# Spilled output products without the residual, and returning outputs on SyncE's queue, in a sparse-attention layer with its FFN

## The chip, the cores and the metric

The kernel runs on one core of a Trainium2 chip. Its time is the device time of one execution in microseconds (us). The time before is the median of 3 runs; a separate execution was taken by the hardware profiler, and its trace gives the rows that are quoted below. Lower is better.

## The reference

For 512 tokens of width 2048 in float32, one layer of a decoder trunk:

```
h = x + nsa_mixer(rmsnorm(x) * mix_g)            # 16 heads of 128, 4 key/value groups
h = h + swiglu(rmsnorm(h) * ffn_g)               # 2048 -> 2 x 5632 -> 2048
out = rmsnorm(h) * final_g
```

The mixer projects the normed tokens, computes for every head a compressed, a selected and a windowed attention with a position bias, adds the three with gates, and multiplies the joined heads by `nsa_w_out` (2048 x 2048). What matters here is the last step: `h = x + o @ nsa_w_out`, with `o` the 16 heads' outputs.

## The kernel before

**Number form.** Every product of two matrices is made from values split into a high part (written by ScalarE in the type that the rows call fp32r) and a low part (the rest, by VectorE): three matmuls for each product (`three`, L267 to L269). So weights arrive as `raw`, ScalarE writes `whi` (L97), VectorE `wlo` (L98). The class `Weights` does this in one fixed order of blocks (512 KB each) with 3 raw buffers: a new raw load may only be issued when VectorE has split an earlier block. During the attention these loads go through the queue of GpSimd (`W.queue = pool`), before and after it through SyncE's.

**The attention.** The loop over heads `h` has 12 steps each. A head's softmax rows (`P`) are scaled and transposed by VectorE in `finish` (L809 to L817), stored to DRAM in four pieces per token block by SyncE (`d_p`, L819), and fetched back turned (`ptr`, L823, SyncE); ScalarE and VectorE split them into `pth` and `ptl` (`turn`, L840 to L844), and TensorE multiplies them with the values (`values`, PSUM tile `o`). While one head is turned and multiplied, the next one's scores are made (`scores`, L802, L804). SyncE's queue also loads the bias rows (`tb`, L773) and stores the outputs of heads 0 to 11 (`d_o`, L865, from the one buffer `stage`).

**The dense stream.** Between the attention's matmuls, `pump` puts matmuls of a generator that runs through the projections of the later heads and then through `partial(0)` to `partial(3)`; the order of every engine's instructions is written by this program. The tiles `hn_h`, `hn_l` first hold the normed input, and, as soon as the last projection `qpair(14)` no longer reads a slice, the outputs of the heads: `reload_o(i)` (L698) loads output `i` from `d_o` into slice `i` of `hn_l`, and `split_o(k)` (L702, L703) splits the slices `2k`, `2k+1`. Reloads 0 to 8 are issued within the last projection, 9 to 11 in the first block of `partial(0)`; splits 0 and 1 come at the end of the projection, 2 to 5 within `partial(0)`.

**The spilled products.** The output projection has 2048 columns. For the first 1024 (`N_SPILL` = 4 chunks of 256), `partial(cb)` multiplies heads 0 to 11 while the last heads' attention still runs. It loads the residual `x` of these columns into `stage` (L712, GpSimd's queue), adds the finished PSUM halves to it (L728, VectorE, eight times in all), and stores the result in DRAM (`d_h`, L729, GpSimd).

**After the attention.** `acc` (512 x 2048) takes `x` for the last 1024 columns (L923) and `d_h` for the first 1024 (L924), both by SyncE. Then heads 0 to 11 are multiplied for the last 1024 columns (two blocks of 512, `cb` 2 and 3, six weight blocks each), added to `acc` (L928), then heads 12 to 15 for all columns, token block by token block, with the second norm (L977) behind each. The feed-forward part follows and takes the rest of the time.

The order around the change is that of the four queues: SyncE issues its transfers in program order and stops at each until what it waits for is there; GpSimd does the same for its own; ScalarE and VectorE work in order.

Of the kernel before, what the change touches and what calls it, by code (L numbers as in the profile page):

```python
# [10 lines left out]
F32 = mybir.dt.float32  # L11
F32R = mybir.dt.float32r
I32 = mybir.dt.int32
AF = mybir.ActivationFunctionType
OP = mybir.AluOpType
# [5 lines left out]
NT, KC = S // 128, D // 128  # L21
# [152 lines left out]
def nsa_block(ctx: ExitStack, tc: tile.TileContext, x, rel_bias, mix_g, ffn_g, fin_g, w_in, w_out,  # L174
              pos_k, w1k, w2k, pos_v, w1v, w2v, f_in, f_out, onehot, out):
    nc = tc.nc
    mm, act, dve, pool = nc.tensor.matmul, nc.scalar.activation, nc.vector, nc.gpsimd
# [17 lines left out]
    hn_h, hn_l = hn_t = [hnp.tile([128, KC, S], F32R, name=f"hn_{x}") for x in "hl"]  # L195
# [3 lines left out]
    d_o = [dram.tile([4, 128, S], F32, name=f"d_o{i}") for i in range(3)]  # L199
    d_h = dram.tile([S, 256 * N_SPILL], F32, name="d_h")  # L200
# [4 lines left out]
    def tok(t):  # L205
        return slice(128 * t, 128 * (t + 1))
# [22 lines left out]
    def rstd(ss):  # L229
        y = smallp.tile([128, 1], F32, name="rs")  # L230
        run(rstd_steps(ss, y))
        return y

    def scaled(src, y, gb, dst):
        for j in range(4):
            c = slice(512 * j, 512 * (j + 1))
            dve.scalar_tensor_tensor(dst[:, c], src[:, c], y, gb[:, c], op0=OP.mult, op1=OP.mult)
# [22 lines left out]
    def turned(xn, js, t):  # L260

        ps = transposed(xn, js, [ps3.tile([128, 512], F32, name="pp") for _ in js])
        his(ps, t, n2_hl)
        los(ps, t, to=n2_hl)

    def three(o, ah, al, bh, bl, start, stop):
        mm(o, ah, bh, start=start, stop=False, skip_group_check=True)  # L267
        mm(o, ah, bl, start=False, stop=False, skip_group_check=True)  # L268
        mm(o, al, bh, start=False, stop=stop, skip_group_check=True)  # L269
# [16 lines left out]
    def run(gen):  # L286
        for _ in gen:
            pass
# [61 lines left out]
    with ExitStack() as st1:  # L350
# [4 lines left out]
        def proj_tiles(n=2):  # L355
            return [(ps1 if next(turns) % 4 > 1 else psx).tile([128, 512], F32, name="proj") for _ in range(n)]
# [5 lines left out]
        with ExitStack() as st0:  # L362
# [28 lines left out]
            def bank(shape):  # L391
                return ps1.tile(shape, F32, name=next(names))
# [49 lines left out]
            p = bank([128, 512])  # L442
            for i in range(N_WARM):
                nc.tensor.transpose(p[:, 128 * (i % 4):128 * (i % 4 + 1)], ident, ident)
            p = bank([128, KC])
# [3 lines left out]
            ps = [bank([128, S]) for _ in range(4)]  # L449
# [5 lines left out]
            ps = proj_tiles()  # L455
            for q in range(4):
# [22 lines left out]
                if q == 3:  # L479
                    p = bank([128, S])  # L480
# [71 lines left out]
        ps = proj_tiles()  # L552
# [3 lines left out]
        ps = proj_tiles()  # L556
# [7 lines left out]
        ps, hk = proj_tiles(), ps1.tile([128, 256], F32, name="mlp")  # L564
# [8 lines left out]
        ps = proj_tiles()  # L573
# [5 lines left out]
        ps, hv = proj_tiles(4), ps1.tile([128, 256], F32, name="mlp")  # L579
        ge = cp.tile([128, NT, 3, H], F32, name="ge")  # L580
        for i in range(8):
# [10 lines left out]
            if i == 1:  # L592
                p = ps1.tile([128, 128], F32, name="tr")
# [16 lines left out]
        ps = proj_tiles()  # L610
# [10 lines left out]
        p = ps1.tile([96, G, 128], F32, name="tr")  # L621
# [8 lines left out]
    with ExitStack() as st2:  # L630
# [13 lines left out]
        def stage_tile():  # L644
            return ap_.tile([128, 1024], F32, name="stage", bufs=1)
# [3 lines left out]
        def proj2():  # L649
            pool_ = (psx, ps2)[next(units) % 2]  # L650
            return [pool_.tile([128, 512], F32, name="proj") for _ in range(2)]
# [43 lines left out]

        def reload_o(i):

            pool.dma_start(hn_l[:, i].bitcast(F32), d_o[i // 4][i % 4])  # L698

        def split_o(k):  # L700
            h, l = (x[:, 2 * k:2 * k + 2] for x in (hn_h, hn_l))
            act(h, l.bitcast(F32), AF.Copy)  # L702
            dve.tensor_tensor(l, l.bitcast(F32), h.bitcast(F32), op=OP.subtract)  # L703

        def partial(cb):
            st = stage_tile().rearrange("p (t c) -> p t c", t=NT)
            c = slice(256 * cb, 256 * (cb + 1))
            ps = [p.rearrange("p (t c) -> p t c", t=2) for p in proj2()]
            for i in range(3):
                w = W.take()  # L710
                if i == 1:
                    pool.dma_start(st, x[:, c].rearrange("(t p) c -> p t c", p=128))  # L712
                for t in range(NT):
                    if not cb and i == 0 and t < 3:
                        reload_o(9 + t)
                    if not cb and i < 2 and t % 2 == 0:
                        split_o(2 + 2 * i + t // 2)
                    if i == 2 and t == 2:
                        W.ahead(3)
                    for k in range(4):  # L720
                        h = 4 * i + k
                        three(ps[t // 2][:, t % 2], hn_h[:, h, tok(t)], hn_l[:, h, tok(t)], w[0][:, k], w[1][:, k],
                              h == 0 and t % 2 == 0, h == 11)
                        if k % 2:
                            yield 650
                    if i == 2 and t % 2:
                        b = t // 2
                        dve.tensor_tensor(st[:, 2 * b:2 * b + 2], st[:, 2 * b:2 * b + 2], ps[b], op=OP.add)  # L728
            pool.dma_start(d_h[:, c].rearrange("(t p) c -> p t c", p=128), st)  # L729
            done["n"] += 1  # L730
            yield None
# [189 lines left out]
    acc = accp.tile([128, NT, D], F32, name="acc")  # L921
    spill = 256 * N_SPILL
    nc.sync.dma_start(acc[:, :, spill:], x[:, spill:].rearrange("(t p) c -> p t c", p=128))  # L923
    nc.sync.dma_start(acc[:, :, :spill], d_h.rearrange("(t p) c -> p t c", p=128))  # L924

    def add(t, cb, p):
        a = acc[:, t, 512 * cb:512 * (cb + 1)]
        dve.tensor_tensor(a, a, p, op=OP.add)  # L928

    def tokmajor(po, w, lhs, first, last, t):  # L930
        for k in range(2):
            lh, ll = lhs(k)
            three(po, lh[:, tok(t)], ll[:, tok(t)], w[0][:, k], w[1][:, k], first and k == 0, last and k == 1)

    def out_tiles():
        return [psx.tile([128, 512], F32, name="proj") for _ in range(2)] + [
            ps3.tile([128, 512], F32, name="po", bufs=2) for _ in range(2)]

    def heads(i):
        return lambda k: (hn_h[:, 2 * i + k], hn_l[:, 2 * i + k])  # L940

    with tc.tile_pool(name="n2", bufs=1) as n2:
        act(warm, epsc, AF.Sqrt)
        gb2 = n2.tile([128, D], F32, name="gb2")
        nc.scalar.dma_start(gb2, ffn_g[0:1, :].to_broadcast([128, D]))
        xn = n2.tile([128, D + 64], F32, name="xn")
        wr_h = n2.tile([128, 6, 1024], F32R, name="wr_h")
        wr_l = n2.tile([128, 6, 1024], F32R, name="wr_l")
        for i in range(6):
            W.place[marks[0] + i] = wr_h[:, i], wr_l[:, i]  # L950
        for cb in (2, 3):
            po = out_tiles()
            for i in range(6):
                w = W.take(2 if cb == 2 else min(2 + i, 6))
                for t in range(NT):
                    tokmajor(po[t], w, heads(i), i == 0, i == 5, t)
            W.ahead(3)
            for t in range(NT):
                add(t, cb, po[t])
        w8 = []  # L960
        for t in range(NT):
            ss = smallp.tile([128, 4], F32, name="ss4")
            po = out_tiles()
            for cb in range(4):
                for i in range(2):
                    if t == 0:
                        w8.append(W.take(7 - len(w8)))
                    tokmajor(po[cb], w8[2 * cb + i], heads(6 + i), i == 0, i == 1, t)
                add(t, cb, po[cb])
                if t == NT - 1 and cb == 3:  # L970
                    W.ahead(3)
                if cb == 3:
                    pool.dma_start(d_r[t], acc[:, t])
                if t and cb in (1, 2):
                    turned(xn, (2 * cb - 2, 2 * cb - 1), t - 1)
                junk = ps3.tile([128, 512], F32, name="pp")
                act(junk, acc[:, t, 512 * cb:512 * (cb + 1)], AF.Square, accum_out=ss[:, cb:cb + 1])  # L977
            scaled(acc[:, t], rstd(ss), gb2, xn)
            W.ahead(min(t, 2))
        pa = [ps3.tile([128, 512], F32, name="pp") for _ in range(2)]  # L980
        gs = []
        for i in range(4):
            gs.append(W.take(min(2, 3 - i)))
            run(ws(pa, i, gs[i], 0, 256, of=n2_hl))
            if i in (1, 2):
                turned(xn, (2 * i - 2, 2 * i - 1), 3)
        act(warm, epsc, AF.Silu)
# [3 lines left out]
    hn_h, hn_l = n2_hl  # L991
# [293 lines left out]
    acc = late.tile([128, NT, D], F32, name="acc")  # L1285
# [171 lines left out]
    c = slice(1536, 2048)  # L1457
# [46 lines left out]
```

## Time and profile before

| | |
|---|---|
| median of 3 runs | 2131.35 us (2129.74 to 2132.30) |
| the profiled execution, its own time | 2133.09 us |
| its span, first to last instruction | 2131.3 us |
| mean granted TensorE clock | 0.995 |
| DMA | 388.08 MB, mean 182 GB/s |
| attention with the dense stream | about 205 to 704 us |
| `partial(0)` to `partial(3)` | about 604 to 699 us |

How to read the rows: in the list of instructions in order of time, each row has the start, the duration, the engine (PE TensorE, PEld its weight loads, DVE VectorE, ACT ScalarE, POOL GpSimd, SP SyncE, with q the queue's own instructions), the line, the operation, result and operands, and, in brackets, how long the engine sat idle before and what ended that. In a table of stretches, each engine has its busy time and the number of instructions, then come the granted TensorE clock, the share of the DMA engines and GB/s. In the list of waits: who waited for whom, total us, times, longest.

### The profile page before, as it was taken

What the parts mean: (1) busy time and instruction counts of PE and PEld (TensorE: products, weight loads), DVE (VectorE), ACT (ScalarE), POOL (GpSimd) and SP (SyncE); (2) the same over time, 40 slices, a digit from 0 to 9 for tenths busy, and PEclk for the clock granted to TensorE, in tenths of its full rate; (3) what the DMA queues carried; (4) which work ended last, traced back from release to release, by engine and by line L of the source; (5) the groups of instructions that cost most, each with busy time, mean ns of one, the idle gap of its engine ahead of it and who ended that gap; (6) DMA issues with size and microseconds to landing.
All of it is one profiled execution on the core that took longest, in us unless ns stands there. A gap on an engine that the chain in (4) does not pass through costs nothing.

```text
span 2131.3 us, 37171 instructions
## 1 busy us (share of the span) xinstructions
PE 2103.4 (99%) x14697; PEld 1950.5 (92%) x14697; DVE 1634.7 (77%) x2674; ACT 928.8 (44%) x1439; POOL 135.2 (6%) x222
## 2 busy tenths in 40 slices
PE   9999999999989999999999999999999999999998
PEld 7898788898979889899999999999999888999996
DVE  5565777777777357898888888888888787877785
ACT  5344455555554234444344343443434444544344
POOL 1000111111121000000000000000000000001000
PEclk9999999999999999999999999999999999999999
DMA  7555767676677633443443434434343786878894
GB/s 223 179 158 148 193 194 197 184 197 188 199 224 229 216 136 109 128 133 117 129 137 113 129 118 129 134 116 130 118 129 129 256 281 219 298 269 313 309 329 147
DMA packets 270331, 388.08 MB, mean 182 GB/s; under 512 B 34155, under 2 KB 202667, under 8 KB 269516
## 3 DMA queue, kind: packets, MB, share of 16 engines
q1 hardware_dynamic: 243820, 273.94, 41.5%
q0 software_dynamic: 24432, 107.56, 14.7%
q10 hardware_dynamic: 1904, 4.20, 0.5%
q8 instruction: 115, 1.88, 0.4%
q14 instruction: 60, 0.49, 0.1%
HBM read 320.52 MB, written 70.36 MB: 183 GB/s over the span
## 4 chain that ended last, share of the span: by engine, by line
PE 66%; DMA 1%; DVE 1%; ACT 1%; issue 0%; SPq 0%; ACTq 0%; DVEq 0%
PE f L267 19%; PE f L268 19%; PE f L269 19%; PE proj L267 1%; PE proj L268 1%; PE proj L269 1%; PE pp L267 1%; PE pp L268 1%; PE pp L269 1%; PE po L267 1%; PE po L268 1%; PE po L269 1%; DMA d_p<-p 1%; DMA rawx<-d_a 0%; PE pp L245 0%
## 5 line engine op out<-in xcount | busy, mean ns | idle before, releaser
L98 DVE TENSOR_TENSOR wlo<-raw,whi 128x1024 fp32r<-128x1024 f32 (+1 forms) x226 | 270.7, 1200 | 115.6 <-ACT whi L97 115.4
L97 ACT ACTIVATE whi<-raw 128x1024 fp32r<-128x1024 f32 (+1 forms) x226 | 234.4, 1040 | 224.4 <-DVE raw L1003 123.0
L1003 DVE TENSOR_TENSOR tlo<-tt,thi 128x1536 fp32r<-128x1536 f32 (+2 forms) x135 | 197.1, 1460 | 108.6 <-ACT thi L1105 88.6
L267 PE MATMUL f<-hn_h,whi 128*128 128x256 f32 x984 | 271.7, 276 | 0.8 <-ACT E L1063 0.8
L268 PE MATMUL f<-hn_l,whi 128*128 128x256 f32 x984 | 271.6, 276 | 0.0
L269 PE MATMUL f<-hn_h,wlo 128*128 128x256 f32 x984 | 271.6, 276 | 0.0
L1100 ACT ACTIVATE whi<-raw 128x1024 fp32r<-128x1024 f32 x123 | 126.1, 1057 | 292.3 <-DVE raw L1003 282.1
L267 PE MATMUL proj<-hn_h,whi 128*128 128x512 f32 x512 | 204.1, 399 | 0.5 <-ACT hn_h L402 0.5
L268 PE MATMUL proj<-hn_l,whi 128*128 128x512 f32 x512 | 200.4, 391 | 0.3 <-DVE hn_l L403 0.3
L269 PE MATMUL proj<-hn_h,wlo 128*128 128x512 f32 x512 | 200.6, 392 | 0.0
L267 PEld LDWEIGHTS f<-hn_h,whi 128*128 128x128 f32 x984 | 184.7, 188 | 1.2 <-ACT E L1063 1.2
L268 PEld LDWEIGHTS f<-hn_l,whi 128*128 128x128 f32 x984 | 184.7, 188 | 0.0
L269 PEld LDWEIGHTS f<-hn_h,wlo 128*128 128x128 f32 x984 | 184.7, 188 | 0.0
L1105 ACT ACTIVATE thi<-tt 128x1536 fp32r<-128x1536 f32 x82 | 121.9, 1487 | 84.0 <-PE f L268 84.0
L269 PE MATMUL proj<-whi,hn_l 128*128 128x256 f32 (+2 forms) x496 | 147.3, 297 | 1.7 <-DVE hn_l L703 1.7
L267 PE MATMUL proj<-whi,hn_h 128*128 128x256 f32 (+2 forms) x496 | 147.7, 298 | 0.9 <-ACT hn_h L702 0.9
L1003 DVE TENSOR_TENSOR wlo<-raw,whi 128x1024 fp32r<-128x1024 f32 x123 | 147.0, 1223 | 0.0
L268 PE MATMUL proj<-wlo,hn_h 128*128 128x256 f32 (+2 forms) x496 | 146.8, 296 | 0.0
L269 PE MATMUL f<-whi,tlo 128*128 128x512 f32 x320 | 125.0, 391 | 0.9 <-DVE tlo L1003 0.9
L268 PE MATMUL f<-wlo,thi 128*128 128x512 f32 x320 | 125.0, 391 | 0.0
L267 PE MATMUL f<-whi,thi 128*128 128x512 f32 x320 | 124.7, 390 | 0.0
L269 PEld LDWEIGHTS proj<-hn_h,wlo 128*128 128x128 f32 x512 | 96.4, 188 | 21.5 <-DVE wlo L98 0.2
(328 smaller groups left out, 6111.6 us busy)
## 6 DMA issues: line engine op xcount, KB each, us to landing
raw<-in_ffn_w_in SPq DMA_DIRECT2D x135, 512.0 KB, 3.7
raw<-in_ffn_w_out SPq DMA_DIRECT2D x88, 512.0 KB, 6.0
rawx<-in_ffn_w_in SPq DMA_DIRECT2D x41, 512.0 KB, 4.9
rawx<-d_a SPq DMA_DIRECT2D x31, 512.0 KB, 4.8
ah<-d_s POOLq DMA_DIRECT2D x16, 896.0 KB, 7.0
al<-d_s POOLq DMA_DIRECT2D x16, 896.0 KB, 9.4
raw<-in_nsa_w_in SPq DMA_DIRECT2D x24, 512.0 KB, 4.8
raw<-in_nsa_w_in POOLq DMA_DIRECT2D x24, 512.0 KB, 5.0
```

What stands on the lines that cost most here:

```text
L97: self.nc.scalar.activation(hi[:, :n], src, AF.Copy)
L98: self.nc.vector.tensor_tensor(lo[:, :n], src, hi[:, :n].bitcast(F32), op=OP.subtract)
L267: mm(o, ah, bh, start=start, stop=False, skip_group_check=True)
L268: mm(o, ah, bl, start=False, stop=False, skip_group_check=True)
L269: mm(o, al, bh, start=False, stop=stop, skip_group_check=True)
L1003: dve.tensor_tensor(o, a, b, op=OP.subtract)
L1100: act(h, r, AF.Copy)
L1105: act(h, ttf, AF.Copy)
```

## The change

Three things change together. `reload_o` issues its twelve loads on SyncE's queue instead of GpSimd's. `partial` no longer loads the residual: ScalarE copies the PSUM halves into `stage`, and `d_h` holds the bare products. After the attention, `acc` takes `x` for all columns; the four spilled chunks are fetched by SyncE into new buffers `back` (three of them) ahead of the third weight block of `cb` 2 and of `cb` 3, two chunks each, and VectorE adds them to `acc` behind that block's own additions.

```diff
         def reload_o(i):
-            pool.dma_start(hn_l[:, i].bitcast(F32), d_o[i // 4][i % 4])
+            nc.sync.dma_start(hn_l[:, i].bitcast(F32), d_o[i // 4][i % 4])
...
             for i in range(3):
                 w = W.take()
-                if i == 1:
-                    pool.dma_start(st, x[:, c].rearrange("(t p) c -> p t c", p=128))
...
                     if i == 2 and t % 2:
                         b = t // 2
-                        dve.tensor_tensor(st[:, 2 * b:2 * b + 2], st[:, 2 * b:2 * b + 2], ps[b], op=OP.add)
+                        act(st[:, 2 * b:2 * b + 2], ps[b], AF.Copy)
             pool.dma_start(d_h[:, c].rearrange("(t p) c -> p t c", p=128), st)
...
-    nc.sync.dma_start(acc[:, :, :spill], d_h.rearrange("(t p) c -> p t c", p=128))
+    nc.sync.dma_start(acc[:, :, :spill], x[:, :spill].rearrange("(t p) c -> p t c", p=128))
...
         for cb in (2, 3):
             po = out_tiles()
+            cs = [slice(256 * c, 256 * (c + 1)) for c in (2 * cb - 4, 2 * cb - 3)]
+            parts = [n2.tile([128, 1024], F32, name="back", bufs=3).rearrange("p (t c) -> p t c", t=NT) for _ in cs]
             for i in range(6):
+                if i == 2:
+                    for c, p in zip(cs, parts):
+                        nc.sync.dma_start(p, d_h[:, c].rearrange("(t p) c -> p t c", p=128))
                 w = W.take(2 if cb == 2 else min(2 + i, 6))
...
             for t in range(NT):
                 add(t, cb, po[t])
+            for c, p in zip(cs, parts):
+                dve.tensor_tensor(acc[:, :, c], acc[:, :, c], p, op=OP.add)
```

## The prediction

> **What bounds the kernel now.** First the page's head, then, from the table of stretches, one at the edits and one behind the attention:
>
> ```profile
> span 2131.3 us, 37171 instructions
> ```
> ```profile
> PE 2103.4 (99%) x14697; PEld 1950.5 (92%) x14697; DVE 1634.7 (77%) x2674; ACT 928.8 (44%) x1439; POOL 135.2 (6%) x222
> ```
> ```profile
> 600.00:620.00 20.00, 14.44 (x77) 12.62 (x76) 15.27 (x32) 9.14 (x22) 4.70 (x8) 0.79 0.76 245
> ```
> ```profile
> 710.00:720.00 10.00, 10.00 (x46) 8.29 (x45) 2.45 (x2) 1.34 (x2) 0.00 (x0) 1.00 1.01 404
> ```
>
> TensorE is busy for 99% of the span: it sets the end, and only its stalls can be won. Behind the stretch's length stand TensorE's busy time and, third from the end, its clock. From 600 to 620 it misses 5.56 us and runs at 0.79 of its clock; behind the attention (710 to 720) it never waits, one matmul of 512 columns starting every 0.22 us (10.00 / 46). Next, the list in order of time. These matmuls start late:
>
> ```profile
> 603.85 0.50 PE L268 MATMUL o<-ptl,v1h 128*128 128x512 f32 x1 [2.90 <-DVE ptl L844]
> ```
> ```profile
> 618.02 0.39 PE L269 MATMUL proj<-whi,hn_l 128*128 128x256 f32 x1 [0.76 <-DVE hn_l L703]
> ```
> ```profile
> 703.20 0.50 PE L855 MATMUL o<-pth,vcc 96*128 96x512 f32 x1
> ```
>
> In the first two TensorE waits for VectorE. What VectorE and ScalarE waited for stands in their own rows:
>
> ```profile
> 597.20 0.63 ACT L840 ACTIVATE pth<-ptr 128x512 fp32r<-128x512 f32 x1 [2.31 <-DMA ptr<-d_p]
> ```
> ```profile
> 597.86 0.69 DVE L844 TENSOR_TENSOR ptl<-ptr,pth 128x512 fp32r<-128x512 f32 x1 [3.84 <-ACT pth L840]
> ```
> ```profile
> 615.65 1.06 ACT L702 ACTIVATE hn_h<-hn_l 128x1024 fp32r<-128x1024 f32 x1 [3.37 <-DMA hn_l<-d_o]
> ```
> ```profile
> 616.75 1.22 DVE L703 TENSOR_TENSOR hn_l<-hn_l,hn_h 128x1024 fp32r<-128x1024 f32 x1 [1.24 <-ACT hn_h L702]
> ```
>
> Two late landings, the fetch `ptr` at 597.20 and reload 7 at 615.65, hold a chain that VectorE works off in order from 597.86 (the second `ptl`, softmax scaling, transposes, splits of heads 0 to 7). In 600 to 620 it is busy for 15.27 of 20 us. TensorE gets on when its links are done, last at 618.02.
>
> **Part 1, reloads on SyncE's queue (L698).** Why is the fetch late? Three times the same four stores and the fetch behind them on SyncE:
>
> ```profile
> 495.12 1.91 SPq L819 DMA_DIRECT2D d_p<-p  x4
> 501.54 0.52 SPq L823 DMA_DIRECT2D ptr<-d_p  x1
> ```
> ```profile
> 584.65 1.93 SPq L819 DMA_DIRECT2D d_p<-p  x4
> 592.71 0.52 SPq L823 DMA_DIRECT2D ptr<-d_p  x1
> ```
> ```profile
> 688.23 2.00 SPq L819 DMA_DIRECT2D d_p<-p  x4
> 696.96 0.52 SPq L823 DMA_DIRECT2D ptr<-d_p  x1
> ```
>
> and what GpSimd issued beside them:
>
> ```profile
> 495.10 0.75 POOL L81 DMA_DIRECT2D raw<-in_nsa_w_in  x1 [9.95 <-DVE ptl L844]
> ```
> ```profile
> 584.93 0.75 POOL L81 DMA_DIRECT2D raw<-in_nsa_w_out  x1 [10.24 <-DVE ptl L844]
> 585.67 1.62 POOL L698 DMA_DIRECT2D hn_l<-d_o  x3
> ```
> ```profile
> 688.00 0.71 POOL L81 DMA_DIRECT2D raw<-in_nsa_w_out  x1 [5.05 <-DVE ptl L844]
> 688.71 0.77 POOL L712 DMA_DIRECT2D stage<-in_x  x1
> ```
>
> The fetch goes out when the stores have landed. With one weight block (512 KB) beside them that takes 6.42 us, with the block and three reloads (768 KB) 8.06, with the block and the residual's load (512 KB) 8.73. In the changed kernel, by the order of its instructions, reloads 0 and 1 stand behind these four stores on SyncE, reload 2 behind the fetch. So I take 6.42: the fetch goes out 1.64 us earlier, at 591.07. It landed 4.49 us after issue. If that stays, the chain starts 1.6 earlier; more than 2.31 it can't, since ScalarE was busy until 594.89. **I take 2.0 us**, between these two; if the reloads hold back the fetch as before, it is 0.
>
> Second, reload 7 was queued on GpSimd behind a weight block that waited for VectorE. On SyncE, 6 and 7 follow the stores of the next token block:
>
> ```profile
> 608.70 0.77 POOL L81 DMA_DIRECT2D raw<-in_nsa_w_out  x1 [4.82 <-DVE wlo L98]
> ```
> ```profile
> 601.03 1.75 SPq L819 DMA_DIRECT2D d_p<-p  x4
> ```
> ```profile
> DMA to landing us min/median/max: 4.3/6.2/7.6
> ```
>
> (the last row: landing times of the twelve reloads). They go out by 604, some 5 us earlier, and at 7.6 us are there by 611.6, in time for ScalarE to split them while VectorE still splits heads 4 and 5 (until 615.51 before, 613.5 now). VectorE's 1.24 us of waiting go (bounds 0 and 1.24): **1.2 us**. TensorE passes the point of 618.02 at 614.8.
>
> What is next: heads 8 to 11, whose reloads now come later. Reloads 9 to 11 stand behind the stores of the block after:
>
> ```profile
> 614.48 1.79 SPq L819 DMA_DIRECT2D d_p<-p  x4
> ```
> ```profile
> 621.90 1.22 DVE L703 TENSOR_TENSOR hn_l<-hn_l,hn_h 128x1024 fp32r<-128x1024 f32 x1
> ```
> ```profile
> 625.02 1.21 DVE L703 TENSOR_TENSOR hn_l<-hn_l,hn_h 128x1024 fp32r<-128x1024 f32 x1
> ```
> ```profile
> 627.04 0.28 PE L269 MATMUL proj<-whi,hn_l 128*128 128x256 f32 x1
> ```
>
> These stores wait for transposes in VectorE's chain, 2.0 us earlier: 612.5 to 614.3, then reload 9. At the shortest landing it is there at 618.6. ScalarE's split takes 1.06 (619.7), and VectorE ends the second of the two splits 4.33 us after it starts the first (621.90 to 626.23): 624.0. TensorE wants it at 627.04 − 3.2 = 623.8. It just holds: **0** (bounds 0 and, at 7.6 us, −3.2). I take the near end because part 1 takes the reloads off the transfers of this time.
>
> Each reload costs SyncE about 0.5 us, 6 us for twelve, with stores, bias loads and fetches of the next head queued behind. This hides it:
>
> ```profile
> SPq L819 <- DVE p L817: 145.9, 39, 8.2
> ```
>
> SyncE stands before stores that VectorE has not finished, 3.7 us each time on average; without that it would cost up to 6. The added wait for TensorE's last reads is over by then:
>
> ```profile
> L268 PE MATMUL proj<-hn_l,whi x32: 387/389/401, 571.8 to 600.1; 128*128 128x512 f32 x32
> ```
>
> Four slices go with each eight of these, so slices 0 to 3 are free by about 579 and 8 to 11 by 593, before the stores that their reloads follow.
>
> **Part 2, no residual in `partial`.** Off: four loads of 512 KB and eight additions on VectorE. On: eight copies on ScalarE, of the shape in which head outputs go to `stage`:
>
> ```profile
> L728 DVE TENSOR_TENSOR stage<-stage,proj x8: 649/682/690, 634.1 to 701.2; 128x512 f32<-128x512 f32 x8
> ```
> ```profile
> L864 ACT ACTIVATE stage<-o x12: 573/576/577, 251.2 to 580.7; 128x512 f32<-128x512 f32 x12
> ```
>
> 8 × 0.58 = 4.6 us on ScalarE, which is idle for half of 600 to 620; 8 × 0.68 = 5.5 us off VectorE. The copies stand where the additions stood and read sums that were ready there; behind them wait the `d_h` stores on GpSimd and the next `pth`, two steps ahead of TensorE. Cost 0; uncovered 4.6. What counts is the end: there, stores to fetch took 8.73 us, now 6.42, so the fetch comes 2.3 earlier.
>
> ```profile
> 699.88 1.67 ACT L840 ACTIVATE pth<-ptr 128x512 fp32r<-128x512 f32 x3 [5.33 <-DMA ptr<-d_p]
> ```
> ```profile
> 699.26 0.34 PE L269 MATMUL o<-pth,v1l 128*128 128x384 f32 x1
> ```
>
> From 699.26 on, TensorE's last seven matmuls could start 0.17 and then 0.22 us apart, the last at 700.8; it started at 703.20, 3.3 us behind the landing (699.88). With the landing at 697.6 it starts at 700.9. **I take 2.0 us** (bounds 0, if the stores are slow for another reason, and 2.4).
>
> **Part 3, behind the attention.** `acc`'s first half no longer waits for `d_h`; on come four loads of 512 KB and four additions of 1024 columns, each as long as this split:
>
> ```profile
> 737.51 1.23 DVE L98 TENSOR_TENSOR wlo<-raw,whi 128x1024 fp32r<-128x1024 f32 x1 [0.41 <-ACT whi L97]
> ```
>
> Two additions (2.46 us) ahead of this split push it to about 740; splits run two blocks of 24 matmuls (10.6 us) ahead of TensorE, which hides it. The other two, at the end of `cb` 3, push one addition whose PSUM tile TensorE wants after 36 more matmuls (7.9 us). VectorE wants the loads only at 737, and SyncE's weight loads behind them are split as far ahead. **0**; uncovered, 4.9.
>
> **Sum.** 2.0 + 1.2 + 0 + 2.0 = 5.2 us off the profiled execution's 2133.09 (span 2131.3): 2127.9. That execution lies 1.74 above the median of 2131.35, so the median comes to **2126.1**.
>
> **A rule against it.** The Trainium skill, "DMA: Bandwidth & Descriptors", section "Issuing engines are not separate DMA queues", says that transfers of all issuers run on the same 16 engines and interleave, so that a second issuer saves only issue time. By it the 2.0 us of part 1 would be 0 and the sum 3.2; rival (a) is this, worked out from the rows alone.
>
> **Rivals.**
>
> (a) *Same transfers, same wait.* The reloads, in whichever queue, delay the stores or the fetch as now. For it: 512 KB stand before the fetch in its own queue. Against: they are issued behind the stores. Part 1 keeps 1.2, the sum is 3.2: **2128.1**. Nearly the same comes out if only the tail's store stays slow (3.2: 2128.1).
>
> (b) *The clock stays up.* The clock behind the stall at 618.02:
>
> ```profile
> 618.00:620.00 2.00, 1.98 (x10) 1.98 (x11) 0.69 (x7) 1.89 (x8) 0.00 (x0) 0.60 0.81 265
> 620.00:622.00 2.00, 2.00 (x12) 2.00 (x11) 1.75 (x3) 2.00 (x5) 0.00 (x0) 0.55 0.07 8
> ```
>
> 0.40 × 2 + 0.45 × 2 = 1.7 us are lost. If the shorter stalls no longer trip it, 6.9 us are won: **2124.4**. Against: the split that ends at 624.0 then holds TensorE. The Trainium skill, "TensorE: Matmul & The Clock Gate", section "Why this matters for your kernels", sets the limit at idle gaps of about 3 us; by it, shorter gaps would not trip the clock, where here one of 0.76 us was followed by half speed.
>
> (c) *Slower: reloads 9 to 11 land late.* In SyncE's queue they stand behind four stores and two fetches. TensorE gets heads 8 to 11 at landing + 5.4, so against before it loses once the landing takes over 7.3 us from 614.3 (621.6 + 5.4 = 627.0). The longest landing of a fetch:
>
> ```profile
> DMA to landing us min/median/max: 2.7/4.4/9.6
> ```
>
> At 9.6 it is 629.3, 2.3 later than before, with another 1.7 at half clock; with nothing won at the tail **2135.4**.
>
> (d) *It does not do what it says*: VectorE's chain is full without the landings, and the time stays: **2131.3**.
>
> **How the numbers follow.** 0.2% of the time (4.3 us; the bound is 2127.1) is about what a measurement of this kernel can tell from no change. Chances: forecast 0.52, (a) 0.28, (b) 0.08, (c) 0.06, (d) 0.06. Faster: nearly all of the forecast and (b), a little of (a): 0.58. Slower by over 0.2%: most of (c): 0.05. Within: 0.37. The range goes from 2124.0, just below (b), to 2130.0, where of the whole sum only the 1.2 of reload 7 is left; it leaves out (c) and (d).
>
> **What would show it.** Right: the fetch near 591, landing near 594.5; no wait of ScalarE for `hn_l` at heads 6 and 7; the last head's L855 within 2 us of the matmul that stands at 699.26 here; TensorE full from 710. Wrong: ScalarE waiting for `hn_l` at heads 8 to 11; stores on SyncE held by reloads; TensorE idle after 735.

## The result and the profile after

The changed kernel takes **2127.55 us** (median of 22 runs, 2126.38 to 2129.9); the kernel before, run beside it, 2131.11 (22 runs, 2128.46 to 2140.49). The ratio is 0.9982, with a 95% interval of 0.9976 to 0.9988: 3.8 us less (2.6 to 5.1), 0.18%, just inside the 0.2% that the prediction took for "no change". The time lies in the range of 2124.0 to 2130.0, between the forecast (2126.1) and rival (a) (2128.1).

The two profiled executions differ by more: 2127.83 against 2133.09, 5.3 us, almost the forecast's sum of 5.2. But the one of before lies 1.98 above its median of 22 runs, the one of after 0.28 above its own. Which of the two differences belongs to the change is what the experiments had to find out.

The head of the page of after, and the stretches that answer to those of before (length, TensorE, its weight loads, VectorE, ScalarE and GpSimd busy, then the clock, the DMA share, GB/s):

```profile
span 2126.1 us, 37171 instructions
```
```profile
PE 2099.3 (99%) x14697; PEld 1947.6 (92%) x14697; DVE 1634.5 (77%) x2670; ACT 932.5 (44%) x1447; POOL 125.8 (6%) x206
```
```profile
600.00:620.00 20.00, 15.82 (x108) 14.61 (x108) 16.48 (x39) 12.22 (x26) 1.50 (x2) 0.91 0.80 259
612.00:614.00 2.00, 2.00 (x10) 1.77 (x11) 1.59 (x7) 0.80 (x5) 0.00 (x0) 0.64 0.94 247
614.00:616.00 2.00, 2.00 (x11) 2.00 (x11) 0.85 (x2) 2.00 (x5) 0.00 (x0) 0.51 0.93 318
...
710.00:720.00 10.00, 10.00 (x45) 8.26 (x45) 1.54 (x3) 2.12 (x2) 0.00 (x0) 1.00 1.02 365
```

TensorE misses 4.18 us of 600 to 620 instead of 5.56, and its clock there is 0.91 instead of 0.79. Behind the attention it is full, as before. Now the fetch, in the list in order of time: SyncE's queue, then ScalarE.

```profile
583.62 1.88 SPq L817 DMA_DIRECT2D d_p<-p  x4
585.54 0.91 SPq L698 DMA_DIRECT2D hn_l<-d_o  x2
589.97 0.52 SPq L821 DMA_DIRECT2D ptr<-d_p  x1
```
```profile
593.95 0.62 ACT L838 ACTIVATE pth<-ptr 128x512 fp32r<-128x512 f32 x1
```

The fetch goes out 6.35 us behind the stores (6.42 was forecast, 8.06 before), and ScalarE does not wait for it. What TensorE waits for now, and the splits behind it:

```profile
600.60 0.50 PE L268 MATMUL o<-ptl,v1h 128*128 128x512 f32 x1 [0.49 <-DVE ptl L842]
602.81 0.38 PE L267 MATMUL proj<-whi,hn_h 128*128 128x256 f32 x1 [0.78 <-ACT hn_h L702]
604.07 0.39 PE L269 MATMUL proj<-whi,hn_l 128*128 128x256 f32 x1 [0.76 <-DVE hn_l L703]
611.98 0.39 PE L269 MATMUL proj<-whi,hn_l 128*128 128x256 f32 x1 [2.15 <-DVE hn_l L703]
```
```profile
607.99 1.99 ACT L702 ACTIVATE hn_h<-hn_l 128x1024 fp32r<-128x1024 f32 x2
```
```profile
610.74 2.32 DVE L703 TENSOR_TENSOR hn_l<-hn_l,hn_h 128x1024 fp32r<-128x1024 f32 x2
```
```profile
617.83 1.06 ACT L702 ACTIVATE hn_h<-hn_l 128x1024 fp32r<-128x1024 f32 x1 [0.66 <-DMA hn_l<-d_o]
```

The wait of 2.90 for `ptl` is down to 0.49. Heads 4 to 7 are split back to back (x2 on both engines): the wait for reload 7 is gone. TensorE now waits 2.15 for the first of these splits, and half clock follows from 612 to 616. Of the late reloads one holds ScalarE for 0.66 (heads 10 and 11), and TensorE waits for none. The tail, and what is new behind it:

```profile
683.28 2.03 SPq L817 DMA_DIRECT2D d_p<-p  x4
690.54 0.52 SPq L821 DMA_DIRECT2D ptr<-d_p  x1
```
```profile
693.38 0.63 ACT L838 ACTIVATE pth<-ptr 128x512 fp32r<-128x512 f32 x1 [1.50 <-PE o L268]
```
```profile
696.51 0.49 PE L853 MATMUL o<-pth,vcc 96*128 96x512 f32 x1
```
```profile
730.34 2.36 DVE L964 TENSOR_TENSOR acc<-acc,back 128x1024 f32<-128x1024 f32 x2
```

Stores to fetch take 7.26 us (8.73 before, 6.42 forecast). The row puts ScalarE's wait of 1.50 down to TensorE, but the fetch landed at 693.28 (2.74 after its issue), and in all fourteen traces below this split starts 0.10 behind that landing: ScalarE still waits for it, 1.50 us instead of 5.33. The last head's matmul (L853 here, L855 in before) follows 3.23 behind the landing (3.43 before). The first two additions to the output are done by 732.7, with TensorE full.

### The profile page after: what moved, and what is told of

Same layout as the page of the kernel before. It is cut to its first block, busy times and chain, and to the rows that moved or that the text cites. A ratio compares the mean times of both kernels' runs of the same rounds, so it can differ in the third digit from the quotient of the medians.

```text
span 2126.1 us, 37171 instructions
## 1 busy us (share of the span) xinstructions
PE 2099.3 (99%) x14697; PEld 1947.6 (92%) x14697; DVE 1634.5 (77%) x2670; ACT 932.5 (44%) x1447; POOL 125.8 (6%) x206
## 4 chain that ended last, share of the span: by engine, by line
PE 68%; DVE 1%; DMA 1%; ACT 1%; issue 0%; ACTq 0%; DVEq 0%
PE f L268 19%; PE f L269 19%; PE f L267 19%; PE proj L267 2%; PE proj L269 2%; PE proj L268 2%; PE pp L267 1%; PE pp L269 1%; PE pp L268 1%; PE po L267 1%; PE po L268 1%; PE po L269 1%; DMA tt<-d_a 1%; PE pp L245 0%; DVE tlo L1008 0%
```

## The experiments

**How they are compared.** Every trace has the same 14,697 matmuls in the same order, so the time between the starts of two of them can be compared across kernels. The *stretch* is that from the 3200th to the 3480th (585.37 to 633.30 in after, 586.22 to 638.76 in before), the *tail* that from the 3960th to the 3990th (692.35 to 699.84, 697.82 to 706.52). Between them, from the 3480th to the 3960th, all fourteen traces take 59.05 to 59.06 us. "To fetch" is the time from the first of the four stores near 584 to the fetch behind them.

| kernel | median us | ratio to before, interval | to fetch | stretch | tail |
|---|---|---|---|---|---|
| before | 2131.11 | | 8.06 | 52.55 | 8.71 |
| before, second trace | | | 7.70 | 50.05 | 8.94 |
| after | 2127.55 | 0.9982, 0.9976 to 0.9988 | 6.35 | 47.93 | 7.50 |
| reloads alone | 2130.10 | 0.9995, 0.9985 to 1.0005 | 6.32 | 48.59 | 10.49 |
| reloads alone, second trace | | | 6.60 | 48.89 | 10.11 |
| residual alone | 2128.72 | 0.9980, 0.9971 to 0.9990 | 7.00 | 49.05 | 7.25 |
| no last residual | 2129.30 | 0.9992, 0.9982 to 1.0001 | 7.73 | 52.35 | 6.97 |
| no adding back | 2127.31 | 0.9977, 0.9969 to 0.9986 | 6.41 | 47.86 | 7.43 |
| first three reloads | 2129.53 | 0.9992, 0.9983 to 1.0001 | 6.23 | 49.67 | 6.92 |
| unused load | 2128.56 | 0.9988, 0.9979 to 0.9996 | 6.45 | 47.96 | 8.00 |
| VectorE copies | 2128.14 | 0.9983, 0.9974 to 0.9992 | 6.45 | 48.53 | 7.03 |
| split earlier | 2130.38 | 0.9994, 0.9984 to 1.0003 | 6.19 | 50.31 | 6.99 |
| split before scores | 2128.48 | 0.9983, 0.9974 to 0.9992 | 6.61 | 48.78 | 7.31 |
| split before scaling | 2128.96 | 0.9989, 0.9980 to 0.9998 | 6.54 | 49.03 | 7.58 |

Each ratio is to runs of before beside it (medians 2131.11 to 2131.79). The intervals are 1 to 2 us to either side, so medians 1 us apart are a hint; what separates the causes is in the last three columns, each from one trace. By the times alone the residual's part (0.9980) cannot be told from the whole change (0.9982): that the reloads add to it stands in the traces only (a stretch of 49.05 against 47.93).

My theory was the forecast's: the reloads' new queue gives 3.2 us between 590 and 620, the residual's removal 2.0 at the tail. The rival: the gain at 590 is not the queue's.

**One part alone: the reloads.** The kernel before with

```diff
-            pool.dma_start(hn_l[:, i].bitcast(F32), d_o[i // 4][i % 4])
+            nc.sync.dma_start(hn_l[:, i].bitcast(F32), d_o[i // 4][i % 4])
```

> The kernel before with the twelve reloads on SyncE's queue and nothing else changed. My theory: the first fetch goes out near 590 and lands near 594, no reload 7 wait, and the time falls by 3.2 us (2.0 of the fetch and 1.2 of reload 7; the trace of the changed kernel would allow up to 4.6, with the half clock that goes): 2126.5 to 2127.9, ratio 0.9978 to 0.9985. Rival (a), transfers delay the fetch whatever queue they stand in: -1.2 us, ratio 0.9994. Rival that the residual's part did it all: 0.

Measured: 1.1 us less (from 3.2 less to 1.1 more). The stretch is what was expected (48.59), but the tail takes 10.49 instead of 8.71. In its trace VectorE's wait for the residual, TensorE's for the last fetch, and two windows behind it:

```profile
692.79 0.69 DVE L728 TENSOR_TENSOR stage<-stage,proj 128x512 f32<-128x512 f32 x1 [1.36 <-DMA stage<-in_x]
```
```profile
697.06 0.49 PE L267 MATMUL o<-pth,v1h 128*128 128x512 f32 x1 [1.31 <-ACT pth L840]
```
```profile
698.00:700.00 2.00, 1.92 (x5) 1.06 (x5) 1.62 (x3) 0.05 (x1) 0.78 (x1) 0.61 0.05 18
700.00:702.00 2.00, 2.00 (x6) 1.57 (x5) 0.69 (x1) 1.30 (x2) 0.00 (x0) 0.54 0.86 270
```

The same wait in before, where the clock stayed up:

```profile
700.56 0.50 PE L267 MATMUL o<-pth,v1h 128*128 128x512 f32 x1 [0.96 <-ACT pth L840]
```

Here it is 1.31, and half clock follows: 0.39 × 2 + 0.46 × 2 = 1.7 us. Much of what was won early is lost at the tail.

**The other part alone: the residual.** The changed kernel with the line above turned back.

> The changed kernel with the reloads back on GpSimd's queue: only the residual's part of the change. My theory: no gain at 590 to 620 (the landing of the fetch stays at 597.2), the last fetch goes out about 1.5 to 2.3 us earlier, nothing is lost behind the attention: -1.5 to -2.0 us, ratio 0.9991 to 0.9993. Rival, the stores of the tail are slow for another reason: 0. Rival, the loads and additions behind the attention cost time: +1 to +5 us.

Measured: 4.3 us less (2.1 to 6.2), by the medians 2.9. The tail came as expected (7.25), but my theory fell at the other place: the stretch takes 49.05, 3.5 less than in before, although the reloads are where they were and nothing of the edit runs ahead of 600. SyncE's and GpSimd's issues there:

```profile
584.79 1.89 SPq L817 DMA_DIRECT2D d_p<-p  x4
...
591.79 0.52 SPq L821 DMA_DIRECT2D ptr<-d_p  x1
```
```profile
592.56 0.76 POOL L81 DMA_DIRECT2D raw<-in_nsa_w_out  x1 [5.03 <-DVE wlo L98]
```

The fetch goes out 7.00 us behind the stores and 0.77 *ahead* of GpSimd's next weight block. In the first trace of before the block went out 0.39 ahead of the fetch at 592.71:

```profile
592.32 0.76 POOL L81 DMA_DIRECT2D raw<-in_nsa_w_out  x1 [5.03 <-DVE wlo L98]
```

So a new theory: where the fetch comes behind the block it lands late, and on GpSimd's queue the two are so close that either comes first. Then the kernel before must show both.

**A second trace of before**, unchanged.

> The kernel before, unchanged: a second trace. My theory: the fetch at 592 goes out 7.0 to 8.1 us behind the stores, close to the issue of GpSimd's next weight block (7.7 us behind them), so that it lands late in some executions and early in others, and the tail loses 1.2 us or more to late portions. If the fetch goes out ahead of the weight block, ScalarE doesn't wait for it and the run is below 2131.6; if behind, ScalarE waits 2 us or more as in the first trace. Rival: the fetch is late in every execution of this kernel.

```profile
583.88 1.88 SPq L819 DMA_DIRECT2D d_p<-p  x4
591.58 0.52 SPq L823 DMA_DIRECT2D ptr<-d_p  x1
```
```profile
591.71 0.76 POOL L81 DMA_DIRECT2D raw<-in_nsa_w_out  x1 [5.03 <-DVE wlo L98]
```
```profile
594.82 0.63 ACT L840 ACTIVATE pth<-ptr 128x512 fp32r<-128x512 f32 x1 [0.55 <-PE proj L269]
```

The fetch is 0.13 ahead of the block and lands 3.13 us after its issue (4.39 in the first trace), the stretch takes 50.05 instead of 52.55, and the time is 2130.66. The row puts ScalarE's wait of 0.55 down to TensorE, to the matmul that ends just before. It was rather the landing, 0.10 before the split starts, as in the first trace. In after, where the fetch landed early, ScalarE starts this split (593.95, above) before the same matmul:

```profile
594.12 0.39 PE L269 MATMUL proj<-hn_h,wlo 128*128 128x512 f32 x1
```

So the fetch is a little late here too. The fourteen traces agree: with the first reloads on GpSimd the fetch was ahead of the block in two (0.13 and 0.77) and behind it in two (0.39, and 0.09 in the run without the last residual). ScalarE waited 2.31 and 2.85 for the landing in the latter, 0.55 with 0.13 ahead, and not at all with 0.77. With the first reloads on SyncE, stores to fetch took 6.19 to 6.61 in ten traces, the fetch was 0.8 to 1.9 ahead and landed 2.6 to 2.9 after its issue, and ScalarE never waited. No run changed the order of the two issues and nothing else, so that the order is the cause is inferred from these fourteen, not shown apart.

**Only the first three reloads on SyncE.** The changed kernel with

```diff
-            nc.sync.dma_start(hn_l[:, i].bitcast(F32), d_o[i // 4][i % 4])
+            (nc.sync if i < 3 else pool).dma_start(hn_l[:, i].bitcast(F32), d_o[i // 4][i % 4])
```

> The changed kernel with only reloads 0 to 2 on SyncE's queue, 3 to 11 back on GpSimd's. With all reloads on GpSimd's queue and no residual (the run of the residual's part alone) the time was about 1.2 us above the changed kernel. My theory: what the queue changes is when the first fetch goes out, 6.3 to 6.4 us behind the stores and so ahead of GpSimd's next weight block, and that comes from the first three alone: the fetch near 590, ScalarE not waiting for it; reload 7 is late again (a wait of 0.5 to 1.2 us on VectorE), so 0.5 to 1.0 us above the changed kernel, ratio 0.9983 to 0.9987. Rival, reload 7 and the later ones are all that counts: the same 1.2 us above the changed kernel with the fetch at 7 to 8 us behind the stores.

The fetch is early (6.23 behind the stores), as expected. But the time is 2.0 us above the changed kernel, more than expected, and the stretch 1.7 (49.67):

```profile
612.40 1.06 ACT L702 ACTIVATE hn_h<-hn_l 128x1024 fp32r<-128x1024 f32 x1 [3.27 <-DMA hn_l<-d_o]
```
```profile
613.50 1.23 DVE L703 TENSOR_TENSOR hn_l<-hn_l,hn_h 128x1024 fp32r<-128x1024 f32 x1 [1.48 <-ACT hn_h L702]
```

Reload 7 holds the chain again, the more the earlier the chain is. Against the residual alone, where the fetch was well ahead of the block by itself, an early fetch gains nothing (49.67 against 49.05); what the queue gives there, 1.1 to 1.7 down to 47.93, is the later reloads', of which reload 7 is the one that is waited for.

**The tail, its load and its additions apart.** The kernel before with the residual's load only for `cb < 3`, and in the last portion ScalarE's copies:

```diff
-                if i == 1:
+                if i == 1 and cb < 3:
                     pool.dma_start(st, x[:, c].rearrange("(t p) c -> p t c", p=128))
```

> The kernel before without the residual's load for the last of the four returning portions (cb 3), whose sums ScalarE copies instead of VectorE adding to them; it leaves out the residual in that quarter of the spilled half. Nothing is moved behind the attention. My theory: the last four stores and the fetch behind them take 6.4 to 7.3 us instead of 8.73, the last head's compressed matmul starts 1.5 to 2.3 us earlier: -1.5 to -2.0 us, ratio 0.9991 to 0.9993. Rival, the tail's stores are slow for another reason: stores to fetch stay at 8.7 us and the time at 0.

Stores to fetch took 6.22 us there, the tail 6.97; 1.7 us less (from 3.8 less to 0.2 more). That trace itself is of a long execution (2134.5, the late fetch among the causes); the tail stands for itself. Next, the changed kernel with the load back, and no additions:

```diff
+                if i == 1 and cb == 3:
+                    for b, part in enumerate([ap_.tile([128, S], F32, name="tb") for _ in range(2)]):
+                        pool.dma_start(part.rearrange("p (t c) -> p t c", t=2),
+                                       x[256 * b:256 * (b + 1), c].rearrange("(t p) c -> p t c", p=128))
```

> The changed kernel with a load of 512 KB for the last portion back in its old place on GpSimd's queue (as two of 256 KB, into tiles that nothing reads), and ScalarE's copies as they are. My theory: the load's transfer delays the last four stores and the fetch behind them, from 7.2 to 8.5 us or more, the last head's matmuls start 1.0 to 1.5 us later, and in some executions the longer stall halves the clock for another 1.8: ratio 0.9987 to 0.9997 (1.2 to 3 us above the changed kernel). Rival: what cost time was VectorE's additions waiting for the residual (2.11 us in the trace of before) and standing between its tail's subtractions: then 0, ratio 0.9982.

```profile
684.07 2.01 SPq L821 DMA_DIRECT2D d_p<-p  x4
692.27 0.52 SPq L825 DMA_DIRECT2D ptr<-d_p  x1
```

8.20 us from stores to fetch, a tail of 8.00, and a median 1.0 above the changed kernel's: the transfer costs 0.5 to 0.8 by itself (against 7.50, and against 7.22, the mean of the nine traces without a load), a little less than expected. The rest of the 8.7 to 10.5 needs the additions too. They alone, as copies on VectorE without any load:

```diff
-                        act(st[:, 2 * b:2 * b + 2], ps[b], AF.Copy)
+                        dve.tensor_copy(st[:, 2 * b:2 * b + 2], ps[b])
```

> The changed kernel with the returning portions copied by VectorE instead of ScalarE: no residual's load, but VectorE's eight operations stand where the additions stood. With the load alone put back for the last portion, the time was 1.0 us above the changed kernel and the tail's thirty matmuls took 8.0 us, against 7.5 in the changed kernel and 8.7 to 10.5 with the load and the additions. Theory: about half of what the residual cost comes from the additions' place in VectorE's order, 0.23 us in two places of the tail and 0.7 to 1 us between 616 and 640 (the stretch took 21.0 us with ScalarE's copies and 21.7 with the additions): +0.7 to +1.5 us against the changed kernel, ratio 0.9985 to 0.9989. Rival: the additions cost only because they waited for the load: 0, ratio 0.9982.

The tail is 7.03, no longer than in the changed kernel, but that hides a cost. The last fetch landed 0.16 behind the 3960th matmul here, earlier than in any other trace (0.38 to 1.03 in the other eight without a load, 1.43 with the load alone, 1.96 and 2.20 in before). From this landing to the last head's matmul it takes 3.56 us; in all nine traces in which ScalarE copies at the tail it is 3.23 or 3.24. So VectorE's operations cost 0.33 there, about the 0.23 in two places that were expected. And the stretch is 0.6 longer (48.53), as expected:

```profile
630.53 0.65 DVE L726 COPY stage<-proj 128x512 f32<-128x512 f32 x1
631.11 1.21 DVE L98 TENSOR_TENSOR wlo<-raw,whi 128x1024 fp32r<-128x1024 f32 x1
632.23 1.02 DVE L842 TENSOR_TENSOR ptl<-ptr,pth 128x384 fp32r<-128x384 f32 x2
```

The first copy stands in the place of the first addition, two operations ahead of a `ptl` for which TensorE waits, and pushes it back by its own 0.6.

**A second trace of the reloads alone**, for the tail.

> The kernel before with the reloads alone moved, a second trace. In the first one the two stretches at 584 to 640 took 48.6 us (52.6 and 50.1 in the two traces of before), but the tail's thirty matmuls took 10.5 (8.7 and 8.9) with the clock at half behind a stall of 1.31 us. Theory: what the reloads win is in every execution, the half clock in the tail only in some; 48.6 us again, and the tail 8.7 to 10.5. Rival: the tail is slower by 1.6 us in every execution of this kernel and takes back what was won.

The tail is 10.11, with the clock at 0.56 and 0.59 behind 698: both traces of this kernel have it, neither of before. The rival stands, as far as two traces go. Why the wait is just long enough there is open: stores to fetch take 8.8 and 9.3, no longer than in before (8.7 and 9.7).

**What adding back costs.** The changed kernel without L956 and L964.

> The changed kernel without the four loads from the spill and the four additions behind the attention; it leaves the spilled half of the sums out of the output. My theory: these are hidden, so the time stays that of the changed kernel, ratio to the kernel before 0.998 (2127.5 us), and the stall of 1.4 us near 1722 is either there too or was chance. Rival: part 3 costs something (its uncovered price is 4.9 us, and the medians gained 1.6 us less than the profiles): 2126 to 2122.6, ratio 0.9960 to 0.9975.

2127.31 against 2127.55: nothing, within 1 us. In the trace of after TensorE waits 1.01 us for VectorE at 1722.20, far behind the change, which would have explained part of the small gain of the medians. It is 0.69 here, 0.26 with the residual alone, and absent with the unused load and with VectorE's copies, which have after's code there: it comes and goes with the same code. Behind the 3990th matmul the eight traces that add back take 1424.4 to 1427.2 us (mean 1425.7), the five that fetch the finished sums 1424.5 to 1425.9 (1425.1): a cost of half a microsecond is not excluded.

**Can the remaining wait be taken?** Three kernels put the split of heads 4 and 5 (2.15 us of waiting at 611.98) earlier on VectorE, and leave it out of its old place in `partial(0)` (a line not shown). First, behind the next head's scores:

```diff
-                    if h0 == H - 2 and i == 3 and n in (0, 3):
+                    if h0 == H - 2 and i == 3 and n in (0, 3, 6):
```

> The changed kernel with the split of heads 4 and 5 put two steps earlier (behind the split of heads 2 and 3, inside the last projection of queries) and that of heads 6 and 7 at the start of the first portion. In the changed kernel's trace TensorE waits 2.15 us for the split of heads 4 and 5 at 611.98 and then runs at half clock for about 3.4 us. My theory: both go, 2.0 to 3.8 us less than the changed kernel, ratio to the kernel before 0.9964 to 0.9973 (about 2124). Rival: VectorE is the bound there, so the work moved ahead delays what stood there (scores and softmax of the next head) by as much, and the same wait comes back at another place: 0 to -1 us against the changed kernel, ratio 0.9977 to 0.9982.

2.8 us above the changed kernel, beyond the rival's worst. That wait is gone, and the next split, of heads 6 and 7, takes its place with 1.47 for its high and 2.38 for its low part:

```profile
612.48 0.39 PE L267 MATMUL proj<-whi,hn_h 128*128 128x256 f32 x1 [1.47 <-ACT hn_h L702]
...
615.37 0.58 PE L269 MATMUL proj<-whi,hn_l 128*128 128x256 f32 x1 [2.38 <-DVE hn_l L703]
```

Second, ahead of the scores:

```diff
-                    if h0 == H - 2 and i == 3 and n in (0, 3):
-                        split_o(n // 3)
+                    if h0 == H - 2 and i == 3 and n in (0, 3, 4):
+                        split_o((n + 1) // 2)
```

> The changed kernel with the split of heads 4 and 5 one step behind that of heads 2 and 3, ahead of the next head's scores on VectorE (in the run with the earlier split it stood behind them and had to wait 1.77 us for ScalarE, which was busy with that head's exponentials). Theory: VectorE has the split done by about 606.5, TensorE's wait of 2.15 us at 611.98 shrinks to 0.5 or less, the half clock behind it goes in most executions, and what stands behind is 1.2 us later without being waited for: 1.5 to 3.3 us less than the changed kernel, ratio 0.9967 to 0.9975. Rival: VectorE's chain is the bound of this stretch, so that the next split or the next fetch is late by the 1.2 us: 0 to +2 us, ratio 0.9982 to 0.9992.

The index is not what the expectation says: it splits heads 4 and 5 twice and heads 2 and 3 not at all, so TensorE's two waits of 0.8 for the latter (at 602.81 and 604.07 above) are absent. VectorE has the same work in the intended order. Even so it is 0.9 above the changed kernel; TensorE waits for the scores' tile instead:

```profile
607.98 0.40 PE L267 MATMUL s<-k1h,qh 128*128 128x288 f32 x1 [2.48 <-DVE mx L800]
```

Third, by one place only, ahead of the softmax scaling:

```diff
                 for n, c in enumerate(last):
+                    if h0 == H - 2 and i == 3 and n == 7:
+                        split_o(2)
                     yield c
```

> The changed kernel with the split of heads 4 and 5 moved by one place only: ahead of the softmax scaling and the transpose that stand before it on VectorE (608.73 to 610.74 in the changed kernel's trace); ScalarE's order stays. The two other places for this split brought nothing or lost. Theory: the split ends near 610.3 instead of 611.96, TensorE's wait of 2.15 us shrinks to about 0.5, the split of heads 6 and 7 ends 0.3 to 0.4 us later and costs TensorE at most 0.7, and the half clock behind 612 goes in some executions: 1.0 to 2.8 us less than the changed kernel, ratio 0.9969 to 0.9977. Rival: the transposes it is put ahead of come 1.5 us later, with them the four stores behind 610.9, the fetch behind 614.5 and reloads 9 to 11, and TensorE waits for one of these: 0 to +2 us against the changed kernel, ratio 0.9982 to 0.9992.

1.4 above the changed kernel. The wait shrinks to 1.37, and what the rival named comes: a `ptl` and a reload late behind the later stores.

```profile
613.95 0.39 PE L269 MATMUL proj<-whi,hn_l 128*128 128x256 f32 x1 [1.37 <-DVE hn_l L705]
620.02 0.33 PE L268 MATMUL o<-ptl,v1h 128*128 128x128 f32 x1 [0.42 <-DVE ptl L844]
```
```profile
619.97 1.06 ACT L704 ACTIVATE hn_h<-hn_l 128x1024 fp32r<-128x1024 f32 x1 [1.07 <-DMA hn_l<-d_o]
```

Three places, three other waits. That points to the sum of VectorE's work as the bound of this stretch, more than its order, but no run takes work off VectorE to show it (it is busy for 16.48 of the 20 us from 600). No version found beats the changed kernel.

## Why the prediction was right in its range and where its steps were off

- **The fetch, 2.0 us** ("I take 2.0 us, between these two"). The mechanism was right, to 0.07 us in the time from stores to fetch. The landing did not stay where the forecast left it: it took 2.7 us from issue instead of 4.4. And the worth was mis-sized, because the wait of 2.31 is not in every execution of before. TensorE's matmul that waits for `ptl` starts 17.6 us into the stretch where the fetch was 0.39 behind the weight block, 15.9 where it was 0.13 ahead, and 15.2 both where it was 0.77 ahead and in after: the earlier fetch is worth 2.4, 0.65 or nothing there.
- **From the execution to the median** ("That execution lies 1.74 above the median"). Here the first error became one of the sum: I treated the 1.74 as a constant of both kernels. By the second trace it belongs to the late fetch of that one execution. That the sum of 5.2 comes so near to the two profiled executions (5.3) is luck: 0.85 of the 5.3 lies ahead of the stretch, before the change begins, 4.6 in the stretch (3.2 forecast), 1.2 at the tail (2.0 forecast), and 1.4 is lost again far behind. The medians differ by 3.6.
- **Rival (a)** comes nearest in time (2128.1), yet not for its reason: the reloads no longer delay the stores as before. The rule behind it (the Trainium skill, "DMA: Bandwidth & Descriptors", "Issuing engines are not separate DMA queues") does not cover this: by it the issuer saves only issue time, but here the fetch that waits for the stores went out 0.4 to 1.9 us sooner (6.19 to 6.61 against 7.00 to 8.06) with the reloads behind the stores in their own queue. Two other things changed with the queue and were not tried apart: two reloads stand there instead of three, and they go out 1.9 us behind the first store instead of 1.0 (585.54 − 583.62, 585.67 − 584.65).
- **Reload 7, 1.2 us**: right. Against the second trace of before, the reloads alone take 1.2 to 1.5 off the stretch.
- **Heads 8 to 11, 0**: right, with 0.66 of waiting on ScalarE and none on TensorE. **SyncE's issue time, 0**: nothing shows a cost; no run tests it by itself.
- **Additions off VectorE, copies on ScalarE, 0**: too low by about 0.6 in the stretch (47.86 to 47.96 in three traces with ScalarE's copies, 48.53 to 48.89 in three with VectorE's operations and the same reloads). I asked what stands behind the copies on ScalarE, and not what stood behind the additions on VectorE: a `ptl` that TensorE waits for.
- **The tail, 2.0 us**: a little too high, 1.2 to 1.7 (8.71 and 8.94 in before; 7.50 in after, and 7.22 in the mean of nine traces without the load, 6.92 to 7.58). The path was right: the last head's matmul hangs on the fetch's landing. Its size was not, as stores to fetch fell to 7.26 and not to 6.42. The cause was only half of it: the load's transfer gives 0.5 to 0.8, the additions' place on VectorE 0.2 to 0.3 behind the landing. With both, the landing itself comes 0.5 to 0.8 later than with the load alone (1.96 and 2.20 against 1.43 behind the 3960th matmul); why is open. With the reloads moved as well, half clock came on top in both traces (10.49 and 10.11).
- **Part 3, 0**: right, as far as half a microsecond can be told.
- **Rival (b), the clock**: half clock between 600 and 622 did not go; it came once, from 612 to 616, instead of twice, and that alone gained nothing that can be seen (below). **Rival (c)**: its late landings did not come.

In executions with the fetch ahead of the block the sum is then 50.05 − 47.93 = 2.1 in the stretch (the queue's 1.2 to 1.5, the rest the additions') and 1.2 to 1.7 at the tail: 3.3 to 3.8, where the medians gave 3.6. The two parts do not add up freely: the reloads alone gain 1.1 (uncertain in sign) because the residual's tail takes back what they win.

## What to carry to other kernels

One profiled execution shows one outcome of every close race between two DMA issues. Where a wait hangs on which of two issues less than half a microsecond apart goes first, take a second trace before pricing it, or price it as a chance; and if the profiled execution lies above the median, ask which of its waits made it so before subtracting that distance from the forecast. A row's name for what ended a wait is inferred: set the landing of the transfer that is read beside it before believing the name. Taking an operation off an in-order engine is worth what stands *behind* it, so look there even when the operation itself waits for nothing.

## What was not expected of the hardware

Half clock came or not behind the same waits, and cost the stretch next to nothing. After and the kernel with the unused load have the same code up to 680 and the same three waits from 600 to 606 (0.49, 0.78, 0.76 and 0.53, 0.78, 0.76). In after the clock stayed up until the wait of 2.15 at 611.98. In the other it fell at once:

```profile
606.00:608.00 2.00, 2.00 (x12) 2.00 (x11) 1.94 (x9) 0.67 (x3) 0.75 (x1) 0.50 0.27 88
608.00:610.00 2.00, 2.00 (x15) 2.00 (x15) 1.26 (x3) 2.00 (x6) 0.00 (x0) 0.75 0.86 297
612.00:614.00 2.00, 1.45 (x12) 1.20 (x10) 2.00 (x3) 0.00 (x0) 0.00 (x0) 1.00 1.05 366
```
```profile
613.19 0.38 PE L269 MATMUL proj<-whi,hn_l 128*128 128x256 f32 x1 [0.55 <-DVE hn_l L703]
```

TensorE came to the split 1.6 us later, waited 0.55 instead of 2.15, and kept its clock afterwards; the stretch took 47.96 against 47.93. Where another engine sets the pace, half clock eats waiting time; at the tail of the reloads alone the clock lost 1.7 us in each trace, and the tail was 1.2 to 1.8 us longer than in before. The Trainium skill ("TensorE: Matmul & The Clock Gate", "What's actually happening") says that activity is judged in free-running windows of 3.4 us, so that where a window begins is left to chance; half clock from 612 to 616 here, which lost 0.36 × 2 + 0.49 × 2 = 1.7 us and so lasted about 3.4, agrees. That an idle window is needed does not: waits of 0.5 to 0.8 in between full work were enough here.
